# Start-up of a two-layer backbone on one core: load order, step list and half w_up splits

## The chip, the cores and the metric

The kernel runs on one NeuronCore of a Trainium2 chip. The metric is device time in microseconds. TensorE (PE) does the matrix products, VectorE (DVE) elementwise work and reductions, ScalarE (ACT) copies, casts and activation functions, GpSimd (POOL) and SyncE (SP) issue transfers. "PEld" is TensorE's weight load, which overlaps its products.

## The reference, cut to what matters

A two-layer backbone over 256 latent and 256 context tokens of width 1024: layer 0 mixes tokens with a chunkwise mLSTM, layer 1 with latent attention, and a gated ConvFFN follows each. Before each sub-layer the tokens are modulated by a shift and a scale that come from a condition vector:

```python
def _modulation(cond, w, b):
    m = jax.nn.silu(cond) @ w + b          # (1024,) @ (1024, 6 * 1024)
    return jnp.split(m[:, None, :], 6, axis=-1)

def _modulate(x, shift, scale):
    return x * (1 + scale) + shift
...
    ml = _modulation(c, ada_w[i], ada_b[i])            # latent tokens
    mc = _modulation(c_ctx[None, :], ada_w[i], ada_b[i])  # context tokens
    hl = _modulate(x, ml[0], ml[1])
    hc = _modulate(xc, mc[0], mc[1])
...
def _mlstm_inputs(h, w_up, ...):
    x_m = h @ w_up                          # (tokens, 1024) @ (1024, 2048)
```

The change touches only the way from the inputs to the first five of the 16 output tiles (128 columns each) of `x_m`. To modulate one feature of the tokens, the whole column of `ada_w` for that feature's shift and scale is needed; to finish any tile of `x_m`, all 1024 features must have been modulated.

## The kernel before, in words

All products are made at fp32 accuracy out of three fp32r products: each operand is *split* into a rounded part `hi`, a cast on ACT (line 389), and a remainder `lo = x - hi`, a subtraction on DVE (line 390). `mm3` (lines 384 to 386) adds hi*hi, hi*lo and lo*hi into one PSUM tile, so its second product needs the remainder of the tokens and its third that of the weights.

The tokens stand transposed: eight tiles `xT[k]` of 128 features by 512 tokens (256 context, 256 latent). The output of w_up is made tile by tile, 128 output features by 512 tokens in one PSUM bank: 8 feature tiles k times three products. Output tiles 0 to 4 (`NUP = 5`) are made in `start_up` while the inputs come in; the others follow in `w_up` (line 699), one at a time, with weights split ahead by the stream (`_split`, lines 323 and 326). The split weights of tiles 0 to 2 lie in the three buffers of tag "w", which the stream reuses for tiles 5, 6 and 7; tile 3's lie in "acc", tile 4's in "u". The evacuation of a tile, `up_evac` (line 681), copies the bank (line 684), splits it, sends it to memory through POOL's queue and starts the convolution (lines 672 to 679).

`start_up` (line 588) issues the loads on SP's queue in the order of `LOADS`: `a0` to `a3` are the four feature groups of the modulation weights (each for two token tiles: 8 transfers of 256 KB into four tiles `adaw` of 128 x 1024), `r0` to `r4` the raw weights of tiles 0 to 4 (512 KB each), `x0` to `x3` two token tiles each (2 x 256 KB). 

Then it emits the steps of `STEPS` inside `manual_schedule` for PE, DVE and ACT: these three engines execute their instructions in exactly the written order, each waiting in place for what it needs. Behind that block, and for SP and POOL throughout, a planner orders instructions by its own costs. The letters before the change:

- `S g`: split all four tiles of group g (`ada_split`; for group 0 the last tile in two halves).
- `A g`: the group's modulation rows (`ada_rows`): 16 products of 512 columns, hi and lo of each k in turn, with the four condition columns as weights (line 478), then the copy of the row tile to SBUF on ACT (line 481).
- `T g`: four small transposes back to columns (line 488). `M g`: add the bias on DVE (lines 498, 499), modulate the group's two token tiles, one half on DVE (line 574) and one on ACT (line 576), and split them (`h_split`).
- `W m`: split the raw weights of tile m (1024 columns, all eight k).
- two digits `g m`: the products of output tile m with the two token tiles of group g.
- `D n`: n products on zeros, into a bank that nobody reads (line 663).

Of the kernel before, what the change touches and what calls it, by code (L numbers as in the profile page):

```python
# [8 lines left out]
F32R = mybir.dt.float32r  # L9
I32 = mybir.dt.int32  # L10
AF = mybir.ActivationFunctionType
ALU = mybir.AluOpType
AX = mybir.AxisListType

D = 1024
# [9 lines left out]
H0 = 4  # L25
H1 = 8
# [3 lines left out]
CW = 1024  # L30

NB, NRAW, NU, NS = 3, 3, 31, 15
# [11 lines left out]

NUP = 5
GROUPS = ((0, 2), (2, 4), (4, 6), (6, 8))
LOADS = [(c[0], int(c[1])) for c in "a0 r0 r1 x0 r2 a1 r3 r4 x1 a2 x2 x3 a3".split()]
STEPS = [(c[0], int(c[1])) for c in (  # L50
    "S0 W0 A0 D3 T0 D6 M0 W1 W2 S1 00 01 W3 W4 A1 03 T1 M1 02 04 10 11 S2 A2 12 T2 M2 13 14 21 "
    "S3 20 A3 24 T3 22 23 M3 31 32 33 34 30").split()]

TAIL = {"mout": 4, "aout": 7, "fout1": 6}
WIDE = {"mout": 5, "aout": 7, "fout1": 10}
# [299 lines left out]
class K:  # L355
# [96 lines left out]
            for c in (2, 5):  # L452
                self.gd[l, c] = self.dr.tile([2, D], F32, name="gd%d%d" % (l, c))

    def ada_split(self, g):
        r = []
        ws = self.adaw.pop(g)
        for w in ws:
            hi, lo = [self.pool.tile([128, 1024], F32R, tag="u", name="adas", bufs=NU) for _ in range(2)]
            n = 512 if g == 0 and w is ws[-1] else 1024  # L460
            for i in range(0, 1024, n):
                self.split(hi[:, i:i + n], lo[:, i:i + n], w[:, i:i + n])
            r.append((hi, lo))
        return r

    def ada_rows(self, g, parts):

        nc = self.nc
        f0, f1 = GROUPS[g]
        nf = f1 - f0  # L470
        n = 256 * nf
        pr = self.ps("adar")
        for i, (hi, lo) in enumerate(parts):
            for kk in range(1024 // n):
                k = i * (1024 // n) + kk
                c = slice(kk * n, (kk + 1) * n)
                for x in (hi, lo):
                    nc.tensor.matmul(pr[0:4, :n], self.condr[:, k, :], x[:, c], start=k == 0 and x is hi,
                                     stop=k == 7 and x is lo)
        r = self.s2("adarow")  # L480
        nc.scalar.copy(r[0:4, :n], pr[0:4, :n])
        return r

    def ada_T(self, g, r):
# [77 lines left out]
        self.bc = None  # L562


    def mod_tiles(self, ks):
        nc = self.nc
        sh, sc = self.modc[0, 0], self.modc[0, 1]
        for k in ks:
            x = self.xT[k]
            for g in range(2):  # L570
                c = 1 - g
                v = x[:, g * 256:(g + 1) * 256]
                if g == 0:
                    nc.vector.tensor_scalar(v, v, sc[:, k, c:c + 1], sh[:, k, c:c + 1], op0=ALU.mult, op1=ALU.add)
                else:
                    nc.scalar.activation(v, v, AF.Identity, bias=sh[:, k, c:c + 1], scale=sc[:, k, c:c + 1])
            if k == 0:
                self.h_split(k)
        for k in ks:
            if k > 0:  # L580
                self.h_split(k)

    def h_split(self, k):
        h = self.u("hT")
# [3 lines left out]
    def start_up(self):  # L588

        nc, st = self.nc, self.st  # L590
        self.hT = []
        self.xcd = self.dr.tile([16, 128, 512], F32, name="xcd")
        self.xmd = self.dr.tile([16, 128, 512], F32, name="xmd")
        self.t2d = {(n, p, j): self.dr.tile([128, 1024], F32, name="t2d")
                    for n, a, b in (("v", 2, 4), ("y", 1, 6)) for p in range(a) for j in range(b)}
        self.xA, self.x1, self.xc, self.xcr = {}, {}, [], []
        w, ps, raws = [], [], []
        src = self.a["ada_w"][0]
        self.adaw, self.xT = {}, []
        for op, g in LOADS:  # L600
            f0, f1 = GROUPS[g] if op != "r" else (0, 0)
            if op == "a":
                wd = 128 * (f1 - f0)
                nk = 512 // wd
                self.adaw[g] = []
                for k in range(8):
                    if k % nk == 0:
                        t = self.uf("adaw")
                        self.adaw[g].append(t)
                    ap = bass.AP(tensor=src.tensor, offset=src.offset + k * 128 * 6 * D + f0 * 128,  # L610
                                 ap=[[6 * D, 128], [D, 2], [1, wd]])
                    c = k % nk * 2 * wd
                    nc.sync.dma_start(t[:, c:c + 2 * wd].rearrange("p (a b) -> p a b", a=2), ap)
            elif op == "x":
                for i in range(f0, f1):
                    x = self.s2("xT")
                    nc.sync.dma_start(x, self.a["tokT"][i])
                    self.xT.append(x)
            else:
                n, _ = st.ids["up", g, 0]  # L620
                r = self.pool.tile([128, 1024], F32, tag="raw" if g < 3 else "ar", name="raw0",
                                   bufs=NRAW if g < 3 else 2)
                nc.sync.dma_start(r, st.ws[n])
                raws.append(r)

        def wsplit(m):
            if m < 3:
                t = self.pool.tile([128, 2, CW], F32R, tag="w", name="w", bufs=NB)
                h, l = t[:, 0], t[:, 1]
            elif m == 3:  # L630
                h, l = [self.pool.tile([128, CW], F32R, tag="acc", name="w0", bufs=2) for _ in range(2)]
            else:
                h, l = [self.pool.tile([128, CW], F32R, tag="u", name="w0", bufs=NU) for _ in range(2)]
            self.split(h, l, raws[m])
            w.append((h, l))
            ps.append(self.ps("up"))

        def part(g, ms):
            for m in ms:
                for k in range(*GROUPS[g]):  # L640
                    c = slice(k * 128, (k + 1) * 128)
                    self.mm3(ps[m], (w[m][0][:, c], w[m][1][:, c]), (self.hT[k][:, 0], self.hT[k][:, 1]),
                             k == 0, k == 7)

        e = mybir.EngineType
        idle = self.ps("idle")
        rows = {}
        with self.tc.manual_schedule(engines={e.PE, e.DVE, e.Activation}):
            for op, g in STEPS:
                if op == "S":  # L650
                    rows[g] = self.ada_split(g)
                elif op == "A":
                    rows[g] = self.ada_rows(g, rows[g])
                elif op == "T":
                    rows[g] = self.ada_T(g, rows[g])
                elif op == "M":
                    self.ada_cols(g, rows.pop(g))
                    self.mod_tiles(range(*GROUPS[g]))
                elif op == "W":
                    wsplit(g)  # L660
                elif op == "D":
                    for _ in range(g):
                        nc.tensor.matmul(idle, self.zero[:, 0:128], self.zero, start=True, stop=True)
                else:
                    part(int(op), [g])
        for m in range(NUP):
            self.up_evac(m, ps[m])

# [30 lines left out]
    def w_up(self):  # L699
        st = self.st  # L700
        for m in range(NUP, 16):
            w = st.use(("up", m, 0))
# [1088 lines left out]
def build(tc, off, a, out):  # L1791
    es = ExitStack()
    with es:
# [4 lines left out]
        k.setup()  # L1798
        st.skip(NUP)
        k.start_up()  # L1800
# [175 lines left out]
```

## Time and profile before

| what | us |
|---|---|
| median of 3 runs (1380.09 to 1381.29) | 1380.56 |
| the profiled execution, whole | 1379.68 |
| its span, first to last instruction | 1377.9 |
| PE busy in the span | 1349.8 |
| PE busy in the first 60.15 us | 50.23 |
| first product of an output tile | 15.98 |

Times in the profile count from the span's start. A row of the timeline gives start, length, engine, line, operation, output and inputs, count; in brackets the idle time before it on that engine and what ended it. Rows with a count are merged: their length is from the first start to the last end.

### The profile page before, as it was taken

The page shows a single profiled execution, that of the slowest core. Times are in us where ns is not written, and L with a number is a line of the kernel's source. Part 1 is how long each engine was busy: PE and PEld are TensorE (multiplying, and loading weights), DVE is VectorE, ACT ScalarE, POOL GpSimd, SP SyncE. Part 2 cuts the span into 40 slices and gives each one's busy share as a digit, 9 for nine tenths or more (in the row PEclk, how much of TensorE's full clock was granted, in tenths as well). Part 3 has the DMA queues.
Part 4 walks back from the last instruction along what each step waited for, and adds up shares of the span by engine and source line. Part 5 has one row for each costly group of instructions (what it writes and reads, how often), then busy time and mean ns, then how long its engine had stood idle before and what let it go on. Part 6 is the DMA issues. An engine that isn't in the chain of part 4 may idle for free.

```text
span 1377.9 us, 18614 instructions
## 1 busy us (share of the span) xinstructions
PE 1349.8 (98%) x6583; PEld 1121.5 (81%) x6583; DVE 1074.9 (78%) x1744; ACT 719.8 (52%) x1238; POOL 121.4 (9%) x215
## 2 busy tenths in 40 slices
PE   7999999999999999999999999999999999999997
PEld 3788888888788888878798888888878888888886
DVE  6599757677588696878789977767888889888873
ACT  6585434445544455364644334334557667466660
POOL 0032000011001011120001000000001001000100
PEclk9999999999999999999999999999999999999999
DMA  9689848789666363766747877746887435356760
GB/s 339 232 294 323 284 153 252 236 288 300 215 196 212 108 230 118 255 194 227 234 139 252 291 243 228 220 144 204 304 252 251 150 100 204 111 185 186 253 201 31
DMA packets 97900, 297.58 MB, mean 216 GB/s; under 512 B 12136, under 2 KB 24808, under 8 KB 97808
## 3 DMA queue, kind: packets, MB, share of 16 engines
q1 hardware_dynamic: 68672, 218.52, 48.7%
q0 software_dynamic: 17472, 57.57, 13.2%
q10 hardware_dynamic: 11664, 20.32, 4.1%
q8 instruction: 51, 0.84, 0.3%
q14 instruction: 41, 0.34, 0.1%
HBM read 262.90 MB, written 33.46 MB: 215 GB/s over the span
## 4 chain that ended last, share of the span: by engine, by line
PE 89%; DVE 5%; ACT 2%; DMA 2%; issue 1%; SPq 0%; ACTq 0%; DVEq 0%
PE fin L1318 8%; PE fin L385 6%; PE fin L384 6%; PE fin L386 6%; PE tok L384 6%; PE tok L385 6%; PE tok L386 6%; PE y L385 5%; PE y L386 5%; PE y L384 5%; PE qk L384 4%; PE qk L386 4%; PE qk L385 4%; PE up L384 2%; PE up L386 2%; PE up L385 2%
## 5 line engine op out<-in xcount | busy, mean ns | idle before, releaser
L326 DVE TENSOR_TENSOR w<-raw,w 128x1024 fp32r<-128x1024 f32 (+3 forms) x290 | 348.0, 1202 | 149.0 <-ACT w L323 142.7
L323 ACT CAST w<-raw 128x1024 fp32r<-128x1024 f32 (+3 forms) x290 | 300.3, 1036 | 287.4 <-PE fin L386 78.9
L516 DVE SCALAR_TENSOR_TENSOR junk<-ar,bc 128x1024 f32<-128x1024 f32 x128 | 155.8, 1217 | 4.1 <-ACT bc L558 1.7
L385 PE MATMUL fin<-h,w 128*128 128x512 f32 (+1 forms) x376 | 141.2, 376 | 0.0
L386 PE MATMUL fin<-h,w 128*128 128x512 f32 (+1 forms) x376 | 140.9, 375 | 0.0
L384 PE MATMUL fin<-h,w 128*128 128x512 f32 (+1 forms) x376 | 140.8, 376 | 0.1
L1318 PE MATMUL fin<-h,w 128*128 128x256 f32 (+1 forms) x640 | 112.9, 339 | 0.0
L1318 PEld LDWEIGHTS fin<-h,w 128*128 128x128 f32 x640 | 98.1, 189 | 14.7
L384 PE MATMUL qk<-xc,w 128*128 128x512 f32 x256 | 100.7, 393 | 0.0
L386 PE MATMUL qk<-xc,w 128*128 128x512 f32 x256 | 99.9, 390 | 0.0
L385 PE MATMUL qk<-xc,w 128*128 128x512 f32 x256 | 99.8, 390 | 0.0
L385 PEld LDWEIGHTS fin<-h,w 128*128 128x128 f32 x376 | 70.8, 188 | 13.1 <-DVE h L1210 0.2
L384 PEld LDWEIGHTS fin<-h,w 128*128 128x128 f32 x376 | 70.6, 188 | 13.2 <-ACT h L1209 0.3
L386 PEld LDWEIGHTS fin<-h,w 128*128 128x128 f32 x376 | 70.8, 188 | 12.6
L384 PEld LDWEIGHTS qk<-xc,w 128*128 128x128 f32 x256 | 48.1, 188 | 10.0 <-issue 0.4
L386 PEld LDWEIGHTS qk<-xc,w 128*128 128x128 f32 x256 | 48.1, 188 | 10.0
L385 PEld LDWEIGHTS qk<-xc,w 128*128 128x128 f32 x256 | 48.1, 188 | 9.7
L384 PE MATMUL up<-hT,w 128*128 128x512 f32 x128 | 50.5, 394 | 0.5 <-ACT hT L389 0.5
L385 PE MATMUL up<-hT,w 128*128 128x512 f32 x128 | 50.1, 392 | 0.4 <-DVE hT L390 0.4
L386 PE MATMUL up<-hT,w 128*128 128x512 f32 x128 | 50.1, 391 | 0.3 <-DVE w L390 0.3
L384 PE MATMUL tok<-w,hT 128*128 128x512 f32 x128 | 49.8, 389 | 0.0
L385 PE MATMUL tok<-w,hT 128*128 128x512 f32 x128 | 49.8, 389 | 0.0
(455 smaller groups left out, 3146.4 us busy)
## 6 DMA issues: line engine op xcount, KB each, us to landing
raw<-in_ws SPq DMA_DIRECT2D x287, 512.0 KB, 4.5
ar<-in_adaT SPq DMA_DIRECT2D x80, 512.0 KB, 4.7
adaw<-in_ada_w SPq DMA_DIRECT2D x32, 256.0 KB, 6.7
t2d<-raw ACTq DMA_DIRECT2D x13, 512.0 KB, 6.0
raw<-t2d SPq DMA_DIRECT2D x13, 512.0 KB, 5.7
raw<-in_ws POOLq DMA_DIRECT2D x13, 512.0 KB, 7.8
zr<-fd ACTq DMA_DIRECT2D x33, 128.0 KB, 4.6
xmd<-xr POOLq DMA_DIRECT2D x16, 256.0 KB, 4.6
```

The lines of the kernel that those rows point to most:

```text
L323: k.nc.scalar.copy(h[:, :cols], src)
L326: k.nc.vector.tensor_sub(l[:, :cols], src, h[:, :cols])
L384: mm(out, w[0], x[0], start=start, stop=False, skip_group_check=on)
L385: mm(out, w[0], x[1], start=False, stop=False, skip_group_check=on)
L386: mm(out, w[1], x[0], start=False, stop=stop, skip_group_check=on)
L516: nc.vector.scalar_tensor_tensor(o, w, 1.0, self.bc[j], op0=ALU.mult, op1=ALU.mult, accum_out=col[:, k, j:j + 1])
L1318: nc.tensor.matmul(o, a, b, start=k == 0 and i == 0, stop=k == 7 and i == 1)
```

## The change

`LOADS` is reordered: group 1 of the modulation weights directly follows group 0, then come the first token tiles and raw weights. Steps become finer. `S g i` splits one tile i of group g, whole, and `A g i` makes the four products of it (hi for both k, then lo for both k); `C g` is the copy of the rows, `T g` the transposes, `O g` the bias; `E k` modulates token tile k and `H k` splits it; `W m i` splits half i of tile m's raw weights (four k); `V k m` is the three products of token tile k for output tile m, and the first and last product of a tile are found by counting. `D n` is as before, with 4 and 3 products where there were 3 and 6. The step lists are the whole order of PE, DVE and ACT. Buffers and tags, and all that follows `start_up`, are the same in the source.

The diff, cut:

```diff
-LOADS = [(c[0], int(c[1])) for c in "a0 r0 r1 x0 r2 a1 r3 r4 x1 a2 x2 x3 a3".split()]
-STEPS = [(c[0], int(c[1])) for c in (
-    "S0 W0 A0 D3 T0 D6 M0 W1 W2 S1 00 01 W3 W4 A1 03 T1 M1 02 04 10 11 S2 A2 12 T2 M2 13 14 21 "
-    "S3 20 A3 24 T3 22 23 M3 31 32 33 34 30").split()]
+LOADS = [(c[0], int(c[1])) for c in "a0 a1 x0 r0 r1 r2 x1 r3 a2 r4 x2 a3 x3".split()]
+STEPS = (
+    "S00 A00 S01 S02 S03 S10 A01 A02 A03 S11 C0 D4 T0 O0 S12 A10 A11 A12 S13 E0 E1 A13 D3 W00 H0 V00 H1 C1 W10 T1 O1 "
+    "V10 W20 E2 E3 H2 V01 H3 V11 V02 W30 W01 S20 W11 S21 V12 V20 V30 S22 V21 V22 V13 S23 V31 V32 W21 A20 A21 A22 W40 "
+    "A23 V23 C2 T2 V14 O2 S30 E4 W31 E5 H4 V03 V33 H5 V04 A30 V24 V40 S31 V50 S32 V51 A31 V41 A32 S33 V42 A33 V52 "
+    "W41 V53 C3 T3 O3 V43 E6 V44 V54 V34 H6 V60 V61 V62 E7 H7 V70 V71 V72 V63 V73 V74 V64").split()
...
+    def ada_split(self, w):
+        hi, lo = [self.pool.tile([128, 1024], F32R, tag="u", name="adas", bufs=NU) for _ in range(2)]
+        self.split(hi, lo, w)
+        return hi, lo
+
+    def ada_mm(self, pr, i, parts):
+
+        for x in parts:
+            for kk in range(2):
+                k = 2 * i + kk
+                self.nc.tensor.matmul(pr[0:4], self.condr[:, k, :], x[:, kk * 512:(kk + 1) * 512],
+                                      start=k == 0 and x is parts[0], stop=k == 7 and x is parts[1])
+
+    def ada_copy(self, pr):
         r = self.s2("adarow")
-        nc.scalar.copy(r[0:4, :n], pr[0:4, :n])
+        self.nc.scalar.copy(r[0:4], pr[0:4])
         return r
...
-        def wsplit(m):
-            if m < 3:
...
+        def wsplit(m, i):
+            if i == 0:
+                if m < 3:
+                    t = self.pool.tile([128, 2, CW], F32R, tag="w", name="w", bufs=NB)
+                    h, l = t[:, 0], t[:, 1]
...
+                w.append((h, l))
+                ps.append(self.ps("up"))
+            c = slice(i * 512, (i + 1) * 512)
+            self.split(w[m][0][:, c], w[m][1][:, c], raws[m][:, c])
...
+                if op == "S":
+                    parts[g, n[1]] = self.ada_split(self.adaw[g][n[1]])
+                elif op == "A":
+                    if n[1] == 0:
+                        rows[g] = self.ps("adar")
+                    self.ada_mm(rows[g], n[1], parts.pop((g, n[1])))
...
+                elif op == "E":
+                    self.mod_tile(g)
+                elif op == "H":
+                    self.h_split(g)
+                elif op == "W":
+                    wsplit(g, n[1])
+                elif op == "V":
+                    k, m = n
                     c = slice(k * 128, (k + 1) * 128)
                     self.mm3(ps[m], (w[m][0][:, c], w[m][1][:, c]), (self.hT[k][:, 0], self.hT[k][:, 1]),
-                             k == 0, k == 7)
...
+                             made[m] == 0, made[m] == 7)
+                    made[m] += 1
```

More of the change, by code (lines that the diff above doesn't have):

```diff
@@ L453, in setup @@
                 self.gd[l, c] = self.dr.tile([2, D], F32, name="gd%d%d" % (l, c))
[L455 to L479, printed above, removed]
+    def ada_split(self, w):
[9 more added lines that the diff above has]
+    def ada_copy(self, pr):
         r = self.s2("adarow")
-        nc.scalar.copy(r[0:4, :n], pr[0:4, :n])
+        self.nc.scalar.copy(r[0:4], pr[0:4])
         return r
@@ L562, in ada_all, with mod_tile @@
         self.bc = None
-    def mod_tiles(self, ks):
+    def mod_tile(self, k):
         nc = self.nc
         sh, sc = self.modc[0, 0], self.modc[0, 1]
[L568 to L581, printed above, removed]
+        x = self.xT[k]
+        for g in range(2):
+            c = 1 - g
+            v = x[:, g * 256:(g + 1) * 256]
+            if g == 0:
+                nc.vector.tensor_scalar(v, v, sc[:, k, c:c + 1], sh[:, k, c:c + 1], op0=ALU.mult, op1=ALU.add)
+            else:
+                nc.scalar.activation(v, v, AF.Identity, bias=sh[:, k, c:c + 1], scale=sc[:, k, c:c + 1])
     def h_split(self, k):
@@ L624, in start_up @@
                 raws.append(r)
-        def wsplit(m):
-            if m < 3:
[L628 to L636, printed above, removed]
@@ L638, in part @@
-        def part(g, ms):
-            for m in ms:
-                for k in range(*GROUPS[g]):
+        def wsplit(m, i):
[3 more added lines that the diff above has]
+                    h, l = t[:, 0], t[:, 1]
+                elif m == 3:
+                    h, l = [self.pool.tile([128, CW], F32R, tag="acc", name="w0", bufs=2) for _ in range(2)]
+                else:
+                    h, l = [self.pool.tile([128, CW], F32R, tag="u", name="w0", bufs=NU) for _ in range(2)]
+                w.append((h, l))
+                ps.append(self.ps("up"))
+            c = slice(i * 512, (i + 1) * 512)
+            self.split(w[m][0][:, c], w[m][1][:, c], raws[m][:, c])
@@ new lines, in start_up @@
+        e = mybir.EngineType
+        idle = self.ps("idle")
+        rows, parts, made = {}, {}, [0] * NUP
+        with self.tc.manual_schedule(engines={e.PE, e.DVE, e.Activation}):
+            for step in STEPS:
+                op, n = step[0], [int(x) for x in step[1:]]
+                g = n[0]
+                if op == "S":
[4 more added lines that the diff above has]
+                    self.ada_mm(rows[g], n[1], parts.pop((g, n[1])))
+                elif op == "C":
+                    rows[g] = self.ada_copy(rows[g])
+                elif op == "T":
+                    rows[g] = self.ada_T(g, rows[g])
+                elif op == "O":
+                    self.ada_cols(g, rows.pop(g))
+                elif op == "E":
[6 more added lines that the diff above has]
+                    k, m = n
@@ L641, in part @@
                     c = slice(k * 128, (k + 1) * 128)
                     self.mm3(ps[m], (w[m][0][:, c], w[m][1][:, c]), (self.hT[k][:, 0], self.hT[k][:, 1]),
-                             k == 0, k == 7)
[L645 to L661, printed above, removed]
+                             made[m] == 0, made[m] == 7)
@@ L662, in start_up @@
+                    made[m] += 1
+                else:
                     for _ in range(g):
                         nc.tensor.matmul(idle, self.zero[:, 0:128], self.zero, start=True, stop=True)
-                else:
-                    part(int(op), [g])
         for m in range(NUP):
```

## The prediction

> **What bounds the kernel now.** I read the page first, then two stretches of the table of busy time per window, then the chain that ended last near the start.
>
> ```profile
> span 1377.9 us, 18614 instructions
> PE 1349.8 (98%) x6583; PEld 1121.5 (81%) x6583; DVE 1074.9 (78%) x1744; ACT 719.8 (52%) x1238; POOL 121.4 (9%) x215
> ...
> 60.00:1350.00 1290.00, 1279.58 (x6266) 1074.02 (x6265) 1023.56 (x1660) 682.74 (x1186) 118.15 (x208) 1.00 0.67 217
> 0.00:60.15 60.15, 50.23 (x209) 30.15 (x210) 37.88 (x57) 35.63 (x49) 0.43 (x5) 1.00 0.81 283
> ...
> 3.70 5.23 DMA adaw<-in_ada_w
> ...
> 24.35 1.23 DVE adas L390
> ...
> 25.62 0.86 PE adar L478 x3
> 26.48 0.23 PE up L384
> ```
>
> PE is the bound. From 60 to 1350 us it is idle for 1290.0 - 1279.6 = 10.4 us; in the first 60.15 us alone, which is what the change rewrites, it is idle for 9.9 us. The chain there runs through the modulation loads, casts and subtractions, and turns into unbroken PE at about 26 us. The change can win only what PE loses before that.
>
> The end of the changed part is the first product of output tile 5:
>
> ```profile
> 26.32 0.39 PE L384 MATMUL up<-hT,w 128*128 128x512 f32 x1
> ...
> 33.84 3.86 PE L478 MATMUL adar<-adas,condr 128*4 128x512 f32 x16
> ...
> 49.81 0.39 PE L386 MATMUL up<-hT,w 128*128 128x512 f32 x1
> 50.13 0.41 PE L488 MATMUL adat<-ident,adarow 4*128 4x4 f32 x4
> 50.46 0.50 PE L384 MATMUL up<-hT,w 128*128 128x512 f32 x1
> 50.80 0.39 PE L385 MATMUL up<-hT,w 128*128 128x512 f32 x1
> ...
> 53.35 0.40 PE L384 MATMUL up<-hT,w 128*128 128x512 f32 x1
> ...
> 60.22 0.39 PE L384 MATMUL up<-hT,w 128*128 128x512 f32 x1
> ```
>
> The 30 products of the last five steps start from 53.35, so tile 5 starts at 60.22 and one product takes 6.87/30 = 0.229 us of PE. A modulation product takes (3.86 - 0.39)/15 = 0.231. A transpose step T costs 50.80 - 49.81 - 2 x 0.23 = 0.53. These three prices rebuild the trace: from 26.32 on there are 108 products (24.7), 32 modulation products (7.4) and three T (1.6), which gives 60.0 against 60.22.
>
> **The loads.** SP issues in the order of LOADS, so arrival is bytes over rate.
>
> ```profile
> 0.00:9.00 9.00, 1.32 (x3) 0.30 (x4) 3.09 (x11) 3.79 (x5) 0.43 (x5) 1.00 0.77 244
> 9.00:14.00 5.00, 4.94 (x20) 1.79 (x18) 4.35 (x5) 3.72 (x5) 0.00 (x0) 1.00 1.05 401
> 15.00:20.00 5.00, 3.79 (x13) 1.74 (x11) 3.13 (x6) 4.33 (x7) 0.00 (x0) 1.00 1.10 350
> 25.00:30.00 5.00, 4.96 (x24) 3.06 (x23) 3.90 (x7) 2.11 (x5) 0.00 (x0) 1.00 1.09 349
> ...
> 7.40 1.04 ACT L389 CAST adas<-adaw 128x1024 fp32r<-128x1024 f32 x1 [0.45 <-DMA adaw<-in_ada_w]
> ...
> 11.70 1.05 ACT L389 CAST w<-raw 128x1024 fp32r<-128x1024 f32 x1 [0.60 <-DMA raw<-in_ws]
> ```
>
> Last column: GB/s. By 9 us 2.20 MB have come. Small constants and group 0 are 2.33 MB, raw tile 0 ends at 2.85 MB; the 0.66 MB left at 401 GB/s end at 10.64, and the cast that waits for it starts at 11.70, so a load is usable 1.06 us after its last byte by this count. Stretches filled by modulation weights (15 to 20 and 25 to 30) run at 350, those of raw tiles and tokens (9 to 14) at 401.
>
> In the new order group 1 directly follows group 0: 4.43 MB, done at 9 + 2.23/0.350 = 15.37, usable at 16.4, where before four other loads stood ahead of it. Then, in pieces of 0.52 MB at 1.31 us: tokens 0 and 1 usable at 17.7, raw 0 at 19.05, raw 1 20.4, raw 2 21.7, tokens 2, 3 at 23.0, raw 3 24.3; group 2 (2.10 MB, 6.0 us) 30.3; raw 4 31.6, tokens 4, 5 32.9, group 3 38.9, tokens 6, 7 40.2. So raw 0 comes 7.4 us later than now.
>
> **The change part by part.** Prices of a split, a modulation and a copy:
>
> ```profile
> 19.49 3.89 ACT L389 CAST adas<-adaw 128x1024 fp32r<-128x1024 f32 x4
> 20.94 4.62 DVE L390 TENSOR_TENSOR adas<-adaw,adas 128x1024 fp32r<-128x1024 f32 x4
> ...
> 26.52 0.58 ACT L481 COPY adarow<-adar 4x512 f32<-4x512 f32 x1 [1.25 <-PE adar L478]
> ...
> 28.73 1.10 ACT L576 ACTIVATE xT<-xT,mod 128x256 f32<-128x256 f32 x2 [1.64 <-DVE mod L499]
> 28.73 0.73 DVE L574 TENSOR_SCALAR xT<-xT,mod 128x256 f32<-128x256 f32 x2
> ...
> 29.73 1.12 ACT L389 CAST hT<-xT 128x512 fp32r<-128x512 f32 x2
> ...
> 30.37 1.29 DVE L390 TENSOR_TENSOR hT<-xT,hT 128x512 fp32r<-128x512 f32 x2 [0.90 <-ACT hT L389]
> ```
>
> A full cast occupies ACT for 0.96 (the last takes 1.05 to land), a full subtraction DVE for 1.14 (1.22); halves take 0.51 (0.61) and 0.60 (0.69).
>
> *Counts.* Five w_up splits become ten halves: 5 x (2 x 0.51 - 0.96) = 0.3 us more ACT, 5 x (2 x 0.60 - 1.14) = 0.3 us more DVE; group 0's last tile is split whole again, which gives 0.06 of each back. Both engines are busy for under two thirds of the 60 us, so I cost this at nothing; without that cover it is 0.3 us. The 64 modulation products and 120 up products are the same. Idle products D go from nine to seven, 0.46 us of PE, all in time that PE waits anyway.
>
> *First product later.* The steps are in order on PE, DVE and ACT. Group 1's last tile: cast 16.4 to 17.5, subtraction 17.5 to 18.7, A13 to 19.4, three idle products to 20.0. ACT meanwhile has done E0 and E1 and waits for raw 0. W00 cast 19.05 to 19.67, H0 cast from 19.56 to 20.2; DVE: W00 subtraction 19.7, H0 subtraction 20.3 to 21.0. So V00's second product starts at 21.0, V00 is done at 21.6, against a first up product at 15.98 now. Behind that wait on raw 0 in ACT's order stand H0, H1 and copy C1, and PE's T1 waits for C1 (20.6 to 21.2): hidden by V00. T1 ends near 22.2.
>
> *But PE then has no break.* At 22.2 remain 39 V steps (117 x 0.229 = 26.8), groups 2 and 3 (32 x 0.231 = 7.4) and T2, T3 (1.1), 35.3 us together: tile 5 would start at 57.5, plus 0.1 for waits below, 57.6. All of groups 0 and 1 is done by then, where now group 1's rows are still worked at 26.
>
> *What hides the operand splits from then on.* Pairs "when the operand is ready / when PE asks for it": V20 25.2/25.9 (H2); V02 23.4/24.3 (W20, whose subtraction stands behind O1 on DVE); A23 32.5/33.6; A33 43.3/45.0; H6 50.3/51.0 (after T3, V43, V44, V54, V34 stand ahead). T2 waits 0.15 for C2, since only V23 covers that copy. The thinnest cover is 0.7 us: a load of tokens 2, 3 or of group 2 later by 0.7 would cost one for one beyond it.
>
> *What it triggers.* SP's loads after x3 (raw tiles for tiles 5 to 7, then two of the later modulation) need buffers freed by W01 (27 us), W11, W21, W31 (38) and W41 (44). The worst order puts the raw tiles behind W41: issued at 44, landed at 48.5 by the page's median for such loads, and the split wants them at 53.4. No POOL issue moves.
>
> ```profile
> raw<-in_ws SPq DMA_DIRECT2D x287, 512.0 KB, 4.5
> ```
>
> **The sum**, against the profiled execution (1379.68 us, span 1377.9): 60.22 - 57.6 = 2.6 us off, 1377.1. The profiled execution is 0.9 below the median 1380.56; from that median 1378.0. This is 0.19%; 0.2% (2.8 us) is about what a measurement of this kernel can tell from no change. PE-bound work behind tile 5 I take to shift whole, since PE idles only 10.4 of 1290 us there, and its loads wait for buffers that its own steps free.
>
> Bounds of the unknowns. Raw 0's time goes one for one: at 340 GB/s and 0.25 us more latency it is 0.5 later (gain 2.1); with group 1 at the 401 of the other loads it is 0.8 earlier (gain 3.4); the stretches of the same weights decide for 350. [...]
>
> **Rivals.**
>
> *The split of tile 5 falls behind evacuations (other side).* Outside the hand-written steps a planner orders ACT. Tile 0 now ends first (V70, 53.4), and frees the buffer for tile 5's split at the same moment.
>
> ```profile
> 54.93 1.06 ACT L323 CAST w<-raw 128x1024 fp32r<-128x1024 f32 x1 [1.83 <-PE up L386]
> ...
> 60.42 0.59 ACT L684 COPY xr<-up 128x512 f32<-128x512 f32 x1 [2.54 <-PE up L386]
> 60.90 0.38 ACT L389 CAST x<-up 128x256 fp32r<-128x256 f32 x1
> 61.16 1.06 ACT L323 CAST w<-raw 128x1024 fp32r<-128x1024 f32 x1
> 62.12 0.78 ACT L672 ACTIVATE cv<-up,sm 128x512 f32<-128x512 f32 x1
> ```
>
> Now two splits run ahead (54.93) because tile 1 frees its buffer first; at 60.42, when tile 0 ends and frees one, copy and cast go first and the split third. By that pattern the split lands at 53.4 + 0.8 + 1.06 + 1.23 = 56.5, 1.1 before PE asks. Were evacuations of three tiles put ahead (3 x (0.59 + 0.38 + 0.78 + 0.64) = 7.2 us by those rows, the last as a cast of 512), the split would land near 62.9 and tile 5 start 2.7 later than now: 1383.3. It decides from 1.1 us of extra work ahead, and slows from 3.7.
>
> *Some of the gain is lost: 1379.0 to 1380.5.* A cover of 0.7 us fails, a wait behind 60 us does not move, or PE's first products go slow again:
>
> ```profile
> 8.26 0.09 PEld L478 LDWEIGHTS adar<-adas,condr 128*4 128x4 f32 x2 [1.18 <-DVE adas L390]
> 8.65 0.12 PEld L478 LDWEIGHTS adar<-adas,condr 128*4 128x4 f32 x1 [0.30 <-issue]
> 9.08 0.12 PEld L478 LDWEIGHTS adar<-adas,condr 128*4 128x4 f32 x1 [0.30 <-issue]
> ```
>
> PE's first products follow each other at 0.43 us (8.65 to 9.08), those later at 0.23. If the waits between 13.4 and 21 us brought that pace back for another 3 us, it would cost about 3 x (1 - 0.23/0.43) = 1.4 us: 1379.4. My working leaves no PE gap over 0.8 us there, so I give this little. [...]
>
> *It gains more, 1375.5 to 1377.6.* The loads come faster with the weights contiguous, or the planner, with three tiles evacuated before tile 5 instead of two splits, shortens some of the 10.4 us behind. For it: DVE idles 22 us in the first 60. Against it: no late wait in the chain belongs to the start.
>
> **How the numbers follow.** The sum as worked out, 2.6 +- 0.6: 0.56 (of it 0.20 beyond 0.2%, 0.36 within). More: 0.18. Some lost: 0.13. Slower: 0.13. So faster 0.38, same 0.49, slower 0.13. The likeliest case's own range is 1377.4 to 1378.6; the range 1375.5 to 1381.5 takes in the gains and the losses up to half of the slower case.
>
> **What would show it.** Right: the first up product near 20 to 21 us with the cast of W00 waiting for the raw load near 19; PE unbroken from 22; tile 5's first product near 57.6; its split's subtraction done before 57. Wrong: an ACT row of tile 5's split that starts after 55.5; a wait of PE on an operand between 22 and 57; or tile 5 early and the gain gone later, to be read as PE idle behind 60 us above 10.4.

## The result and the profile after

The changed kernel takes 1397.68 us (median of 4 runs) against 1380.32 (4 runs): ratio 1.0129, 95% interval 1.0117 to 1.0142. Forecast was 1378.0, a gain of 2.6; it is 17.4 us slower.

The start-up does what was worked out, nearly. From the timeline of the changed kernel, ACT's and DVE's rows at the end of the step list, and PE's first product of tile 5:

```profile
54.41 0.59 ACT L678 COPY xr<-up 128x512 f32<-128x512 f32 x1 [2.31 <-PE up L389]
54.89 0.38 ACT L392 CAST x<-up 128x256 fp32r<-128x256 f32 x1
55.16 1.06 ACT L326 CAST w<-raw 128x1024 fp32r<-128x1024 f32 x1
...
56.25 1.23 DVE L329 TENSOR_TENSOR w<-raw,w 128x1024 fp32r<-128x1024 f32 x1 [0.52 <-ACT w L326]
...
58.39 0.41 PE L387 MATMUL up<-hT,w 128*128 128x512 f32 x1
```

Tile 0 ends first, ACT copies and casts it and splits tile 5 third; that split lands at 57.5. The copy at 54.41 waits for V70; six steps of three products follow V70, and the product at 58.39 is the one after them: tile 5 starts 1.8 us earlier than at 60.22. So the loss lies behind it: 1396.3 - 58.39 = 1337.9 us from there to the end of the span, against 1377.9 - 60.22 = 1317.7 before, 20.2 more for the same instructions in the same order.

The page and the windows (core, PE busy and its instructions, PEld, DVE, ACT, POOL, PEclk, DMA share, GB/s) of the changed kernel:

```profile
span 1396.3 us, 18622 instructions
PE 1371.9 (98%) x6581; PEld 1125.3 (81%) x6581; DVE 1077.6 (77%) x1748; ACT 720.4 (52%) x1242; POOL 121.1 (9%) x215
...
60.00:1350.00 1290.00, 1282.01 (x6161) 1060.94 (x6160) 1015.52 (x1650) 671.37 (x1175) 116.54 (x206) 1.00 0.66 216
...
100.00:300.00 200.00, 200.00 (x862) 162.36 (x861) 137.86 (x184) 90.79 (x137) 21.51 (x38) 1.00 0.74 247
```

PE is not idle more: 8.0 of 1290 us, where it was 10.4. It is busy more with the same work. From 100 to 300 us it has no gap and does 862 products; before, in the same stretch:

```profile
100.00:300.00 200.00, 200.00 (x884) 165.67 (x883) 143.61 (x191) 93.40 (x140) 22.09 (x39) 1.00 0.77 254
```

That is 200/862 = 0.2320 us per product against 200/884 = 0.2262, 2.6% slower at the same granted clock, 1.00. Below, the time from one product's start to the next one's is called the *pitch*. Which products are slower is seen in the groups (operation, tiles, count, busy us, mean ns, idle before). Before:

```profile
L386 PE MATMUL tok<-w,hT 128*128 128x512 f32 x128 | 49.8, 389 | 0.0
L386 PE MATMUL tok<-w,s 128*128 128x512 f32 x96 | 37.2, 389 | 0.0
L386 PE MATMUL av<-v,PT 128*128 128x512 f32 x48 | 18.7, 389 | 0.0
```

After:

```profile
L389 PE MATMUL tok<-w,hT 128*128 128x512 f32 x128 | 50.6, 395 | 0.0
L389 PE MATMUL tok<-w,s 128*128 128x512 f32 x96 | 37.7, 395 | 0.0
L389 PE MATMUL av<-v,PT 128*128 128x512 f32 x48 | 18.7, 390 | 0.0
```

Products that read a split stream weight (tile w) are slower, in layers and lines that the change does not touch; the attention values (av), whose operands both lie in tag u, are not. What do all the slower ones share? The places of the buffers in SBUF, as the two programs list them (byte address in a partition, of a tag's first buffer):

```
tag                            before    after
u     (tokens, activations)     39200    39200
w     (split stream weights)   186656   186784
8-column tiny tiles            211232   186656
```

The pool gives a tag its place when the source first claims it. Before, step W0 claims tag w ahead of M0, whose bias tile is the first of the tiny tag. In the new list O0 claims the tiny tag (4 buffers of 32 bytes) ahead of W00: w slides 128 bytes on, and no other tag that PE reads moves. The distance from u to w goes from 147456, a multiple of 256, to 128 more than one.

### The profile page after: what moved, and what is told of

Same layout as the page of the kernel before. It is cut to its first block, busy times and chain, and to the rows that moved or that the text cites. A ratio compares the mean times of both kernels' runs of the same rounds, so it can differ in the third digit from the quotient of the medians.

```text
span 1396.3 us, 18622 instructions
## 1 busy us (share of the span) xinstructions
PE 1371.9 (98%) x6581; PEld 1125.3 (81%) x6581; DVE 1077.6 (77%) x1748; ACT 720.4 (52%) x1242; POOL 121.1 (9%) x215
## 4 chain that ended last, share of the span: by engine, by line
PE 90%; DVE 3%; DMA 3%; ACT 2%; issue 1%; SPq 0%; ACTq 0%; DVEq 0%
PE fin L1312 8%; PE fin L387 6%; PE fin L389 6%; PE fin L388 6%; PE tok L387 6%; PE tok L389 6%; PE tok L388 6%; PE y L388 5%; PE y L389 5%; PE y L387 5%; PE qk L387 4%; PE qk L389 4%; PE qk L388 4%; PE up L387 2%; PE up L388 2%; PE up L389 2%
## 5 line engine op out<-in xcount | busy, mean ns | idle before, releaser
L388 PE MATMUL fin<-h,w 128*128 128x512 f32 (+1 forms) x376 | 143.2, 381 | 0.0
L389 PE MATMUL fin<-h,w 128*128 128x512 f32 (+1 forms) x376 | 143.0, 381 | 0.0
L387 PE MATMUL fin<-h,w 128*128 128x512 f32 (+1 forms) x376 | 142.8, 381 | 0.1
L387 PE MATMUL qk<-xc,w 128*128 128x512 f32 x256 | 102.0, 399 | 0.0
L389 PE MATMUL qk<-xc,w 128*128 128x512 f32 x256 | 101.3, 396 | 0.0
L388 PE MATMUL qk<-xc,w 128*128 128x512 f32 x256 | 101.2, 395 | 0.0
```

Source lines behind the costliest of these rows:

```text
L387: mm(out, w[0], x[0], start=start, stop=False, skip_group_check=on)
L388: mm(out, w[0], x[1], start=False, stop=False, skip_group_check=on)
L389: mm(out, w[1], x[0], start=False, stop=stop, skip_group_check=on)
```

## The experiments

**The address, given back and taken away.** Theory "address" against the rival "order". e1 claims the first w buffer ahead of the steps; e2 leaves the kernel before as it is but claims the tiny tag first:

```diff
 e1, on the changed kernel
+        w_first = self.pool.tile([128, 2, CW], F32R, tag="w", name="w", bufs=NB)
         def wsplit(m, i):
...
-                    t = self.pool.tile([128, 2, CW], F32R, tag="w", name="w", bufs=NB)
+                    t = w_first if m == 0 else self.pool.tile([128, 2, CW], F32R, tag="w", name="w", bufs=NB)
 e2, on the kernel before
         idle = self.ps("idle")
+        nc.vector.memset(self.tiny(8, "adt"), 0.0)
```

> The changed kernel, with the first split-weight buffer claimed before the step list, so that tag w gets the address it has in the kernel before (186656 in place of 186784); steps, loads and sizes are the changed kernel's. Theory 'address': the 17 us come only from the place of the split weights, which are 128 bytes further on; products follow each other at 0.227 us again (0.232 to 0.233 in the changed kernel) and the time is 1380.3 - 2.6 = 1377.7, the start-up gain that was predicted. Rival 'order': the new step order leaves a slower state of PE or of the instruction streams whatever the addresses; 1397.7, pitch 0.232.

> The kernel before, its steps and loads untouched; only the small tag of 32-byte tiles is claimed ahead of tag w (one memset, 0.06 us), so that w lies at 186784 as in the changed kernel while tag u stays. Theory 'address': 1380.3 + 20 = 1400, pitch 0.232. Rival 'order': 1380.4, pitch 0.227.

e1 took 1377.06 us against 1379.74 for the kernel before: ratio 0.9982 (0.9972 to 0.9991). e2 took 1401.6: 1.0162 (1.0142 to 1.0182). The window from 100 to 300 us (columns as above), of e1 and then of e2:

```profile
100.00:300.00 200.00, 200.00 (x884) 165.68 (x883) 143.72 (x189) 93.15 (x138) 21.45 (x37) 1.00 0.76 256
```

```profile
100.00:300.00 200.00, 200.00 (x862) 162.18 (x861) 140.45 (x192) 92.63 (x140) 23.36 (x41) 1.00 0.74 248
```

The whole loss follows the address in both directions, by 20.6 us in the new steps (1397.68 to 1377.06) and 21.9 in the old. Counted from tile 5's first product to the end, which leaves out a start-up that differs by more than 1 us between executions, the profiles give 20.6 us (1337.9 against e1's 1317.3) and 19.7 us (1337.4 in e2 against 1317.7 before). "Order" is out. And with the address given back the change is worth 2.7 us, as forecast.

**Place or distance.** A pad ahead of tag u moves u and w together:

```diff
 e3 (128 bytes: 32 columns), e4 (32 bytes: 8 columns), on the kernel before
+        pad = p.tile([128, 32], F32, name="pad")
+        nc.vector.memset(pad, 0.0)
         self.mod0 = p.tile([128, 2, 8, 2], F32, name="mod0")
```

> The kernel before with a pad of 128 bytes ahead of tag u, so that u and w both lie 128 bytes further on, and their distance stays. If the distance between the two operands of a product decides ('distance'): 1380.4, pitch 0.227. If the place of each alone decides ('place'): 1400 or more, pitch 0.232 or slower.

> The kernel before with a pad of 32 bytes ahead of tag u: u and w move together by 32 bytes and begin on a multiple of 64 (39232 and 186688), which no operand of these tags does now. 'Distance': 1380.4, pitch 0.227. 'Place', in the form that rows which begin inside a 64-byte line cost an extra line: faster, 33 lines become 32, a pitch of 0.220 and some 30 us less.

e3: 1379.72 (ratio 1.0004, 0.9994 to 1.0014), w at 186784 as in the changed kernel. e4: 1380.62 (1.0010, 1.0000 to 1.0021). Both show 884 products from 100 to 300 us, as before the change; e3's row:

```profile
100.00:300.00 200.00, 200.00 (x884) 165.62 (x883) 144.01 (x193) 95.19 (x142) 23.06 (x40) 1.00 0.76 255
```

Neither the place alone (e3) nor a start on a multiple of 64 bytes (e4) moves the median by more than 0.1%; the distance between u and w does, by 1.6% in e2. The extra line of 64 bytes in e4's expectation was the author's guess: some 30 us less did not come.

**The price by itself.** m1 leaves the whole reference out, as its expectation says, and runs products alone:

```diff
+        def group(name, du, dw):
+            ps = psp.tile([128, 512], F32, tag="ps", name=name)
...
+                    u = [U[:, k * 1024 + du + h * 512:k * 1024 + du + (h + 1) * 512] for h in range(2)]
+                    w = [W[:, h * 1024 + dw + k * 128:h * 1024 + dw + (k + 1) * 128] for h in range(2)]
...
+                    mm(ps, w[0], u[0], start=s, stop=False)
+                    mm(ps, w[0], u[1], start=False, stop=False)
+                    mm(ps, w[1], u[0], start=False, stop=e)
```

> Computes none of the reference: it writes zeros to the output and runs only products, 17 groups of 48 (three per 128-row block, weights 128 columns out of W, 512 moving columns out of U, both with the token data in them), each group with U and W begun some bytes further on (u32 = 32 bytes); first with DVE and ACT idle (A), then the same groups with casts and subtractions of 128x1024 running beside (B). If two operand streams of PE itself get in each other's way ('distance'), the pitch is 0.226 to 0.227 in A at w0 and w512 and 0.232 at w128, and the same at u128 w128 as at u0 w0. If it takes the other engines' traffic ('contention'), A shows one pitch for all and only B differs. If the place of either alone decides, u128 w128 differs from u0 w0.

The run has 19 groups in each part, not 17; the first and the last are both without added bytes. Rows of two groups in part A (line, operation, tile and count; min, median and max ns; first and last start), the first with W begun 128 bytes on, the second with none:

```profile
L1825 PE MATMUL A_u_w__330<-U,W x16: 390/393/404, 63.2 to 73.7; 128*128 128x512 f32 x16
```

```profile
L1825 PE MATMUL A_u_w__1016<-U,W x16: 389/389/389, 217.7 to 227.9; 128*128 128x512 f32 x16
```

From the first to the last start of line 1825 a group has 45 products. With the starts to a hundredth (63.20 to 73.66 and 217.72 to 227.92 here) the pitch in us, by bytes added to U and W (they begin a multiple of 256 apart; the value for 0, 0 is the last group's, since the start of the first is mixed with the warm-up group):

```
U, W           pitch     U, W           pitch     U, W           pitch
0, 0           0.2267    0, 192         0.2291    0, 512         0.2271
0, 32          0.2331    0, 224         0.2336    32, 32         0.2271
0, 64          0.2333    0, 256         0.2267    64, 64         0.2273
0, 96          0.2340    0, 320         0.2333    128, 128       0.2276
0, 128         0.2324    0, 384         0.2327    128, 0         0.2324
0, 160         0.2333    0, 448         0.2291    256, 0         0.2278
```

In part B, with casts and subtractions beside, every group has the same pitch to 0.0001. So it is PE's own two operands. The values at 0 and 256, 64 and 320, 128 and 384, 192 and 448 agree within 0.0003: over the distances tried here they repeat every 256 bytes. Off a multiple of 256 a product costs 2.5 to 3.2% more in m1, with less, 1.1%, at 192. "Contention" and "place" are out.

**Other distances in the kernel.** e5, e6 and e7 are e1 with a pad of 256, 64 and 32 bytes ahead of w (`pad = self.pool.tile([128, n], F32, name="pad")` and a memset, ahead of `w_first`).

> As e1_w_first, with a pad of 256 bytes ahead of tag w (distance of u and w 256 more than a multiple of 512). 'Distance': another pitch than 0.2262; if it grows with the distance from a multiple of 512, 0.232 or more, 1397 or later. 'Place': unknown.

> As e1_w_first, with a pad of 64 bytes ahead of tag w. 'Distance', if it grows evenly to 128: pitch 0.229, about 1387; if any distance but a multiple of 512 costs the same: 1397.

> As e1_w_first, with a pad of 32 bytes ahead of tag w. 'Distance', if even: pitch 0.2277, about 1382; if any distance costs the same: 1397.

They took 1377.23, 1392.37 and 1400.71 (ratios 0.9979, 1.0093, 1.0153 to 1379.17). Products between 100 and 300 us, of e5, e6 and e7:

```profile
100.00:300.00 200.00, 200.00 (x884) 165.62 (x883) 142.84 (x189) 92.74 (x138) 21.51 (x37) 1.00 0.77 254
```

```profile
100.00:300.00 200.00, 200.00 (x873) 163.79 (x872) 140.16 (x186) 91.82 (x138) 21.54 (x38) 1.00 0.74 249
```

```profile
100.00:300.00 200.00, 200.00 (x859) 160.71 (x858) 137.29 (x183) 90.26 (x137) 21.71 (x38) 1.00 0.73 246
```

The price neither grows with the distance nor is it the same for every distance: e7, the smallest, costs most, e6 less, and 256 is as good as none. This fits m1, since some products have w as weights and u moving and others the reverse: the reverse of 32 is 224, and both are dear in m1; the reverse of 64 is 192, the cheapest. e6's trace agrees: where w holds the weights (fin<-h,w) the pitch is 0.2333, where w moves (tok<-w,hT) 0.2289, against 0.2270 and 0.2267 in e1.

By the count of products, m1's prices give too much. In e6's program 2450 products of 512 columns stand at 64 and 1969 at 192: 2450 x 0.0066 + 1969 x 0.0024 = 20.9 us, measured 15.3 over e1. For the changed kernel 4319 more products of 512 stand at 128 than before: 4319 x 0.0057 = 24.6, measured 20.6 (e1) and 21.9 (e2). That is 12 to 37% too much. The traces of e1 and of the changed kernel, read product by product behind the start of tile 5, show where it goes: 3741 products that followed within 0.230 us in e1 take 22.9 us more at 128, which is 0.0061 each, but 540 that already took longer in e1 give 2.1 us back. So these 540 do not pay the price on top; what makes them long was not found. In e6 the 565 such products likewise give 1.3 us back instead of paying.

**What carries the start-up gain.** e8 is the kernel before with the new LOADS line; e9 is e1 with the old LOADS line; e10 is e1 with each w_up weight split whole:

```diff
 e10, on e1: the steps W01, W11, W21, W31 and W41 are taken out of the list, and
-            c = slice(i * 512, (i + 1) * 512)
+            c = slice(0, 1024)
```

> The kernel before with the new LOADS alone. The prediction's working (each engine in the written order, loads by bytes over 350 and 400 GB/s) puts tile 5 at 67.1 instead of 60.2, because W0 stands ahead of A0 in the old steps and waits for raw 0 at 19: 1379.7 + 6.9 = 1386.6. If the loads carry the gain by themselves: 1377.

> e1_w_first with the old LOADS: the new steps alone. By the same working the first product waits for group 1's weights, which land behind raw 0 to 2 and tokens 0 and 1, till 25, and tile 5 starts at 62.5: 1379.7 + 2.3 = 1382.0. If the finer steps carry the gain by themselves: 1377.

> e1_w_first with w_up weights split whole, at the place of the first half. By the same working V00's operands are ready 0.5 later and V01 and V02 wait for whole splits: tile 5 at 59.1 in place of 57.6, 1.5 us more than e1: 1378.6. If halves are worth nothing: 1377.1.

Against 1379.53: e8 1387.01 (ratio 1.0057, 1.0039 to 1.0076), e9 1382.67 (1.0025, 1.0015 to 1.0035), e10 1378.85 (0.9995, 0.9987 to 1.0004). ACT's row in e8, and in e9 the first cast of group 1:

```profile
19.63 1.04 ACT L389 CAST w<-raw 128x1024 fp32r<-128x1024 f32 x1 [7.99 <-DMA raw<-in_ws]
20.58 0.57 ACT L481 COPY adarow<-adar 4x512 f32<-4x512 f32 x1
```

```profile
17.70 1.04 ACT L392 CAST adas<-adaw 128x1024 fp32r<-128x1024 f32 x1 [5.73 <-DMA adaw<-in_ada_w]
```

In e8 ACT stands 8 us before W0, with the copy of group 0's rows behind it; in e9 a wait of 5.7 us stands before group 1. Each half of the change by itself loses (7.5 and 3.1 us), both together gain 2.7. e10 is 1378.85 - 1377.06 = 1.8 us slower than e1, though measured at another time and on another chip.

The three times are near the expectations, but the start-ups are not quite: tile 5 begins at 67.75, 63.77 and 60.88, where 67.1, 62.5 and 59.1 were expected. In all three profiles PE's products stand at 0.43 us for some time, as its first ones did before the change. In e10 (rows of PE, then a window):

```profile
25.32 0.63 PE L388 MATMUL up<-hT,w 128*128 128x512 f32 x1
25.75 0.63 PE L389 MATMUL up<-hT,w 128*128 128x512 f32 x1
...
24.00:28.00 4.00, 4.00 (x11) 3.14 (x12) 3.55 (x8) 2.95 (x6) 0.00 (x0) 0.57 1.09 350
```

The granted clock there is 0.57; in e8 and e9 it is 0.50 from 20 to 24 us, behind waits of PE of 6.8 and 5.2 us; what sets it is not shown. Against e1, e10's tile 5 is 3.1 us late: 0.9 from raw 0, which landed later, 1.0 from the whole split ahead of V00, and 1.3 from the slow products less a wait that only e1 has. So the 1.8 us is not the price of halves alone, and e10's nearness to its expectation is in part luck.

**Tag s2 into step too.**

```diff
 e11, on e1
+        pad = p.tile([128, 32], F32, name="pad")
+        nc.vector.memset(pad, 0.0)
         jp = p.tile([128, 128], I32, tag="s2", name="jp", bufs=NS)
...
+        pad2 = p.tile([128, 32], F32, name="pad2")
+        nc.vector.memset(pad2, 0.0)
         self.mod0 = p.tile([128, 2, 8, 2], F32, name="mod0")
```

> e1_w_first with two pads of 128 bytes, ahead of tag s2 and ahead of tag u, so that s2, u and w all begin 32 bytes past a multiple of 256 (s2 stands 128 off u and w in all kernels so far). Counted in the program, 44 products of 512 columns, 72 of 256 and 132 transposes go from distance 128 to 0. By the 0.0057 us per product of m1 that is at least 0.25 us, with the smaller ones at the same price 1.4: 1375.6 to 1376.8. If only products with split stream weights mind: 1377.1.

e11 took 1376.77 (ratio 0.9980, 0.9971 to 0.9989). It lies within the first range, but 0.3 us under e1 is less than these runs can tell. e1, e5 and e11 beat both kernels, and no difference between them is shown.

## Why the prediction was right and wrong

*Wrong: "PE-bound work behind tile 5 I take to shift whole."* The step that failed is that this work keeps its length. It took 1317.7 us before and 1337.9 in the changed kernel, because a product there takes 0.2320 us in place of 0.2262 (100 to 300 us). That price follows the distance between two buffers (0.2262 again in e1 and e3, 0.2320 in e2), and the change moved one of them. I read from the diff that buffers and tags are the same, which is true of their sizes and not of their addresses: those follow the order in which tags are claimed, and the order is what the change rewrites. No case among the rivals had it: the slower one (1383.3) was another mechanism. Nor did a sign of being wrong: the loss was looked for as idle time of PE behind 60 us, and that fell from 10.4 to 8.0 us.

The profile before held both prices, though only the addresses tell which product has which. Tile 3's weights lie in "acc", 128 bytes off a multiple of 256 from u: behind 26.3 us its 24 products follow at 0.232 by their median, the other 84 at 0.227, and the 0.229 of the prediction is a mix. The 18 products qr<-w,cqT stand at 128 before and run at 0.232; the change puts these on a multiple of 256, where they run at 0.227. One line of them, before and after (columns as in the rows of m1):

```profile
L384 PE MATMUL qr<-w,cqT x6: 390/394/505, 1099.0 to 1102.6; 128*128 128x512 f32 x6
```

```profile
L387 PE MATMUL qr<-w,cqT x6: 388/390/501, 1116.3 to 1119.9; 128*128 128x512 f32 x6
```

*Right: the start-up.* With the address given back it can be read without the other effect. e1's rows:

```profile
9.00:14.00 5.00, 4.75 (x17) 1.76 (x15) 4.20 (x4) 3.65 (x4) 0.00 (x0) 1.00 1.08 352
...
16.42 1.05 ACT L392 CAST adas<-adaw 128x1024 fp32r<-128x1024 f32 x1 [0.40 <-DMA adaw<-in_ada_w]
...
19.05 0.62 ACT L392 CAST w<-raw 128x512 fp32r<-128x512 f32 x1 [0.58 <-DMA raw<-in_ws]
...
21.05 0.50 PE L388 MATMUL up<-hT,w 128*128 128x512 f32 x1 [0.31 <-DVE hT L393]
...
40.84 0.19 PEld L388 LDWEIGHTS up<-hT,w 128*128 128x128 f32 x1 [0.47 <-DVE hT L393]
...
53.85 0.59 ACT L680 COPY xr<-up 128x512 f32<-128x512 f32 x1 [2.24 <-PE up L389]
...
54.60 1.06 ACT L326 CAST w<-raw 128x1024 fp32r<-128x1024 f32 x1
...
57.78 0.39 PE L387 MATMUL up<-hT,w 128*128 128x512 f32 x1
```

Group 1 was forecast usable at 16.4: 16.42. Raw 0 at 19.05: 19.05. V00's second product at 21.0: 21.05. Tile 5 at 57.6: 57.78, counted from V70 as above. Behind it e1 takes 1317.3 us, so that at the old distance this work does shift whole. The gain in time was to be 2.6 us, measured 2.7.

That it fits to a few hundredths is luck. In the eight profiles with the new load order raw 0 is usable between 19.05 and 20.21, and e1's is the earliest; with the old loads and steps it is between 11.70 and 12.99 in four, and the one that the working started from is the earliest. The measured gain, from the medians of 10 and 25 executions, does not hang on it.

One thing was left out: at 40.85 e1's PE waits 0.3 us for the subtraction of H5, ahead of V50, a pair that the prediction's list of covers does not have. So PE was not quite unbroken from 22.

The rate of the loads was right too: group 1 came at 352 GB/s in e1 (9 to 14 us), near the 350 that the sum used.

*The rivals.* Evacuations ahead of tile 5's split: it came third, behind copy and cast, as the pattern before said, with its cast from 54.60 in e1 (forecast about 54.2). Slow products (0.43 us) again behind the first ones: not in e1 and the changed kernel, whose granted clock is 1.00 from 6 to 60 us, but in e8, e9 and e10, at 1.6 us in e10, where the prediction had said about 1.4. That it gave this little, for want of a PE gap over 0.8 us, agrees with the trace before: behind a wait of 0.84 us its products follow at 0.23 (three from 22.22 take 0.85 us). What sets the slow pace is not shown: the granted clock is 0.57 in e10, but 1.00 in the trace before from 8 to 10 us, where products stand at 0.43 too. More gain: no.

*The changed kernel's own start* lies 0.6 later than e1's (58.39 against 57.78). Its raw 0 was usable 0.57 later in the execution that was profiled:

```profile
19.62 0.62 ACT L392 CAST w<-raw 128x512 fp32r<-128x512 f32 x1 [0.59 <-DMA raw<-in_ws]
```

This lies within the spread above. The lag is there from group 0's third tile on (cast at 9.58 against 8.98), ahead of every product of an output tile; why loads differ so between executions is not shown. From raw 0 to tile 5 it is 38.77 us against 38.73 in e1: the dearer products add about 0.3 us, an estimate from this and from e1's wait of 0.3 us at 40.85, which the changed kernel does not have.

## What to carry to other kernels

Where a pool places buffers in the order in which the source claims them, any reordering of steps can move operands. Compare addresses before and after a change, and fix the order of claims where it matters; e1, e3, e4 and e5, which keep u and w a multiple of 256 bytes apart, all keep the fast pitch (884 products from 100 to 300 us, 0.2262 us each). If PE has no more idle time and yet takes longer at the same granted clock, count products per stretch: a pitch that shifts in untouched stages, here by 2.6%, pointed in this case to the operands and not to the schedule. The reorder of loads and the reorder of steps each lost alone (7.5 and 3.1 us) and gained together (2.7 us at the old distance), so such a pair should be judged as one.

## What the runs showed of the hardware

In m1, for fp32r products with 128 weight columns and 512 moving columns, the pitch followed the distance in SBUF from the start of the moving operand to the start of the weights, modulo 256 bytes: 0.2267 to 0.2278 us at 0, 0.2291 at 192, 0.2324 to 0.2340 at the other multiples of 32 that were tried. The place of the pair changed it by no more than 0.0011 us, casts and subtractions beside by no more than 0.0001. In this kernel, where 4319 such products went to another distance, 128 bytes were worth 21 us; 677 shorter products of 256 to 384 columns, which went there too, took 0.6 us more together. The granted clock shows nothing of it: it is 1.00 from 100 to 300 us in the kernels and, in m1, from 0 to 425 us.

Why the distance matters was not found. m1 changes all its distances together, so it does not tell whether a product's own weights count or the next one's, loaded while it runs (before the change PEld is busy for 81% of the span and PE for 98%). Other types were not measured, nor shorter moving operands alone.
